# Row-wise largest absolute value of an 8192 x 8192 matrix: GpSimd's shares in two parts, the last row in six pieces, and a store moved to another queue

## Chip, cores, metric

One core of one Trainium2 chip. The metric is the device time of one execution in microseconds (us). Kernels are compared only within the same rounds. A ratio is the mean time of one kernel's fast runs over that of the other's of the same rounds, so it is not quite the ratio of the medians that are quoted.

## The reference

```
x: 8192 x 8192 float32, normally distributed
return np.linalg.norm(x, ord=np.inf, axis=1)      # as used here: the largest |x| of each row
```

The kernel reads 268 MB once and writes 32 KB.

## The kernel before

"Row" below means 128 rows of the matrix, one to each SBUF partition: 8192 columns of float32 on 128 partitions, 4 MB. There are 64 of them: two single ones, 30 pairs, and two single ones at the end. Loads go through a ring of three pairs' size. VectorE reduces each load by itself, except in the last pair and the last two rows: there a share goes to ScalarE (absolute value, in place) and then GpSimd (a maximum over the bits as integers). Each entry of the list is (columns of the piece, columns of them for ScalarE and GpSimd).

```
TILES = (
    [[(8192, 0)]] * HEAD
    + [[(16384, 0)]] * (PAIRS - 1)
    + [[(16384, 7328)], [(8192, 3488)]]
    + [[(4128, 1824), (2048, 864), (1024, 416), (512, 0), (480, 0)]]
)
...
    def absmax_pool(dst, src):
        keep(nc.scalar.activation(src, src, mybir.ActivationFunctionType.Abs))
        max_pool(dst, src)
...
            load = nc.sync.dma_start(out=buf, in_=src[:, off : off + w]).ins
...
            if final:
                pairs_out()                      # two copies on ScalarE, then the store from ScalarE's queue
                absmax(res[:, R - 1 :], last)    # last piece and all partial results of the row
            elif u == len(TILES) - 1:
                for eng, a, e in ((absmax, 0, w - g), (absmax_pool, w - g, w)):
                    ...
                        warm(red, WARM.get(h, ()))   # products that nothing reads
...
    nc.tensor.transpose(ps_ones, res[:, X_ONE:], ident)
    keep(nc.scalar.copy(sb_ones, ps_ones))
    keep(nc.scalar.dma_start(
        out=out[X_ONE * P :].rearrange("(r p) -> r p", p=P), in_=sb_ones
    ))
```

The results of the 60 paired rows are transposed and stored while the last row comes in; those of the four single rows follow at the end: one transpose on TensorE (PE), one copy, one store.

Of the kernel before, what the change touches and what calls it, by code (L numbers as in the profile page):

```python
# [8 lines left out]
P = 128  # L9
FP32 = mybir.dt.float32  # L10
INT32 = mybir.dt.int32
MAX = mybir.AluOpType.max
X = mybir.AxisListType.X



# [2 lines left out]
HEAD = 2  # L19
PAIRS = 30  # L20
TILES = (
    [[(8192, 0)]] * HEAD
    + [[(16384, 0)]] * (PAIRS - 1)
    + [[(16384, 7328)], [(8192, 3488)]]
    + [[(4128, 1824), (2048, 864), (1024, 416), (512, 0), (480, 0)]]
)
RING = 3 * 16384

# [1 line left out]
WARM = {-2: (4, 4, 4), -1: (4,), 0: (4,), 1: (2,)}  # L30


@with_exitstack
def kernel(
    ctx: ExitStack,
    tc: tile.TileContext,
    x: bass.AP,
    out: bass.AP,
):
    nc = tc.nc  # L40
    n_rows, n_cols = x.shape
    R = n_rows // P
    assert R == 64 and n_cols == 8192

    X_ONE = 2 * PAIRS
    n_ones = R - X_ONE
    keep = tc.keep_in_program_order

    single = ctx.enter_context(tc.tile_pool(name="single", bufs=1))
    psum_pool = ctx.enter_context(tc.tile_pool(name="psum", bufs=1, space=bass.MemoryType.PSUM))  # L50

    ring = single.tile([P, RING], FP32)
    res = single.tile([P, R], FP32)
    ident = single.tile([P, P], FP32)


    n_part_last = sum((w > g) + (g > 0) for w, g in TILES[-1][:-1])
    w_last = TILES[-1][-1][0]
    last = single.tile([P, w_last + n_part_last], FP32)

    ps_warm = psum_pool.tile([P, 4 * P], FP32)

    def absmax(dst, src):
        return keep(nc.vector.tensor_reduce(  # L64
            out=dst, in_=src, axis=X, op=MAX, apply_absolute_value=True,
        )).ins

    def max_pool(dst, src):

        pool = nc.gpsimd  # L70
        keep(pool.add_instruction(  # L71
            mybir.InstTensorReduce(
                name=nc.get_next_instruction_name(),
                ins=[pool.lower_ap(src.bitcast(INT32))],
                outs=[pool.lower_ap(dst.bitcast(INT32))],
                op=MAX,
                axis=X,
            )
        ))

    def absmax_pool(dst, src):
        keep(nc.scalar.activation(src, src, mybir.ActivationFunctionType.Abs))  # L82
        max_pool(dst, src)

    def setup(after):

        tc.add_manual_dep(
            nc.gpsimd.memset(ident, 0.0).ins, after.name,  # L88
            mybir.DependencyInfo(mybir.DependencyClass.Sync, mybir.DependencyReason.DATA),
            reason="not before the first row is in",  # L90
        )
        make_identity(nc, ident, nomemset=True)

    def load_table(after):

        abs_ident = nc.scalar.activation(  # L96
            ident[:, :1], ident[:, :1], mybir.ActivationFunctionType.Abs
        )
        tc.add_manual_dep(
            keep(abs_ident).ins, after.name,  # L100
            mybir.DependencyInfo(mybir.DependencyClass.Sync, mybir.DependencyReason.DATA),
            reason="not before the second row is in",
        )

    def warm(after, widths):

        for w in widths:
            product = keep(nc.tensor.matmul(  # L108
                ps_warm[:, : w * P], lhsT=ident,
                rhs=ident.unsqueeze(1).to_broadcast([P, w, P]), start=True, stop=True,  # L110
            )).ins
            tc.add_manual_dep(
                product, after.name,
                mybir.DependencyInfo(mybir.DependencyClass.Sync, mybir.DependencyReason.DATA),
                reason="not before this piece",
            )

    ps_pairs = [psum_pool.tile([PAIRS, P], FP32, name=f"ps_pairs{r}") for r in range(2)]

    def transpose_pairs():  # L120
        both = res[:, :X_ONE].rearrange("p (g r) -> p g r", r=2)
        for r in range(2):
            keep(nc.tensor.transpose(ps_pairs[r], both[:, :, r], ident))  # L123

    def pairs_out():
        sb = single.tile([PAIRS, P, 2], FP32, name="sb_pairs")
        for r in range(2):
            keep(nc.scalar.copy(sb[:, :, r], ps_pairs[r]))  # L128
        keep(nc.scalar.dma_start(
            out=out[: X_ONE * P].rearrange("(g p r) -> g p r", p=P, r=2), in_=sb  # L130
        ))


    loads = []
    at = 0
    next_pair, next_one = 0, X_ONE
    for u, pieces in enumerate(TILES):
        k = sum(w for w, _ in pieces) // n_cols
        if k == 2:
            row, next_pair = next_pair, next_pair + 2  # L140
        else:
            row, next_one = next_one, next_one + 1
        src = x[row * P : (row + k) * P].rearrange("(p r) m -> p (r m)", r=k)
        off = 0
        n_part = 0
        for h, (w, g) in enumerate(pieces):
            final = u == len(TILES) - 1 and h == len(pieces) - 1
            if final:
                buf = last[:, :w]
            else:  # L150
                if at + w > RING:
                    at = 0
                buf = ring[:, at : at + w]
                at += w
            load = nc.sync.dma_start(out=buf, in_=src[:, off : off + w]).ins  # L155
            if not final:
                if (len(loads) + 4) % 10 < 5:


                    for a, v, earlier in loads:  # L160
                        if a < at and at - w < a + v:
                            tc.declare_no_dep(
                                load, earlier, reason="ordered by the reduces in between",
                            )
                loads.append((at - w, w, load))
            off += w
            if u == len(TILES) - 1 and h == 0:
                transpose_pairs()
            if final:
                pairs_out()  # L170
                absmax(res[:, R - 1 :], last)
            elif u == len(TILES) - 1:
                for eng, a, e in ((absmax, 0, w - g), (absmax_pool, w - g, w)):
                    if a < e:
                        i = w_last + n_part
                        red = eng(last[:, i : i + 1], buf[:, a:e])
                        n_part += 1
                        if eng is absmax:
                            warm(red, WARM.get(h, ()))
            elif g == 0:  # L180
                red = absmax(
                    res[:, row : row + k], buf.rearrange("p (c m) -> p c m", m=n_cols)
                )
                if u == 0:
                    setup(red)
                elif u == 1:
                    load_table(red)
            else:

                part = single.tile([P, 2], FP32, name=f"part{u}")  # L190
                c = w // n_cols - 1
                if c:
                    absmax(res[:, row : row + c], buf[:, : c * n_cols])
                red = absmax(part[:, 0:1], buf[:, c * n_cols : w - g])
                absmax_pool(part[:, 1:2], buf[:, w - g :])
                max_pool(res[:, row + c : row + c + 1], part)
                warm(red, WARM[u - len(TILES) + 1])

    ps_ones = psum_pool.tile([n_ones, P], FP32)
    sb_ones = single.tile([n_ones, P], FP32)  # L200
    nc.tensor.transpose(ps_ones, res[:, X_ONE:], ident)  # L201
    keep(nc.scalar.copy(sb_ones, ps_ones))  # L202
    keep(nc.scalar.dma_start(
        out=out[X_ONE * P :].rearrange("(r p) -> r p", p=P), in_=sb_ones
    ))


# [28 lines left out]
```

## Time and profile before

| | before |
|---|---|
| time, median of the first runs | 628.18 us (628.06 to 628.35) |
| execution that the profile shows | 628.7 us, span 626.92 us |
| load rate over the span | 428 GB/s |
| last pair usable for ScalarE / last reduce starts / ends / span ends | 603.80 / 623.62 / 624.28 / 626.92 us |

The span is what the profile shows of the execution; the time was 1.77 to 1.81 us longer in each execution for which both are known. The profile's page and the chain of waits are read in the prediction below.

### The profile page before, as it was taken

What the parts mean: (1) busy time and instruction counts of PE and PEld (TensorE: products, weight loads), DVE (VectorE), ACT (ScalarE), POOL (GpSimd) and SP (SyncE); (2) the same over time, 40 slices, a digit from 0 to 9 for tenths busy, and PEclk for the clock granted to TensorE, in tenths of its full rate; (3) what the DMA queues carried; (4) which work ended last, traced back from release to release, by engine and by line L of the source; (5) the groups of instructions that cost most, each with busy time, mean ns of one, the idle gap of its engine ahead of it and who ended that gap; (6) DMA issues with size and microseconds to landing.
All of it is one profiled execution on the core that took longest, in us unless ns stands there. A gap on an engine that the chain in (4) does not pass through costs nothing.

```text
span 626.9 us, 203 instructions
## 1 busy us (share of the span) xinstructions
PE 8.8 (1%) x15; PEld 3.3 (1%) x15; DVE 537.1 (86%) x39; ACT 14.7 (2%) x10; POOL 13.5 (2%) x13
## 2 busy tenths in 40 slices
PE   0000000000000000000000000000000000000005
PEld 0000000000000000000000000000000000000002
DVE  1938988889888899888898888988889888899888
ACT  0000000000000000000000000000000000000044
POOL 0000000000000000000000000000000000000007
PEclk9999999999999999999999999999999999999999
DMA  9999999999999999999999999999999999999997
GB/s 370 433 468 401 468 401 443 427 414 456 406 464 401 468 401 468 401 468 401 468 401 468 401 468 401 468 401 468 401 468 401 447 422 439 431 414 456 401 435 303
DMA packets 5525, 268.47 MB, mean 428 GB/s; under 512 B 627, under 2 KB 789, under 8 KB 1045
## 3 DMA queue, kind: packets, MB, share of 16 engines
q1 hardware_dynamic: 5472, 268.44, 99.2%
q10 hardware_dynamic: 53, 0.03, 0.0%
HBM read 268.44 MB, written 0.03 MB: 428 GB/s over the span
## 4 chain that ended last, share of the span: by engine, by line
DMA 70%; DVE 29%; SPq 0%; issue 0%; PE 0%; ACT 0%; DVEq 0%
DMA ring<-in_x_dram 70%; DVE res L64 28%; DVE part L64 1%; DVE last L64 1%; SPq L155 0%; PE ps_ones L201 0%; ACT sb_ones L202 0%; DVEq L64 0%
## 5 line engine op out<-in xcount | busy, mean ns | idle before, releaser
L64 DVE TENSOR_REDUCE res<-ring 128x2 f32<-128x16384 f32 (+1 forms) x32 | 525.4, 16419 | 87.0 <-DMA ring<-in_x_dram 87.0
L82 ACT ACTIVATE ring<-ring 128x7328 f32<-128x7328 f32 (+4 forms) x5 | 12.6, 2523 | 577.0 <-DMA ring<-in_x_dram 577.0
L71 POOL TENSOR_REDUCE part<-ring 128x1 int32<-128x7328 int32 (+1 forms) x2 | 9.4, 4697 | 587.9 <-ACT ring L82 587.9
L108 PE MATMUL ps_warm<-ident 128*128 128x512 f32 (+1 forms) x12 | 8.3, 836 | 614.5 <-DVE part L64 613.5
L108 PEld LDWEIGHTS ps_warm<-ident 128*128 128x128 f32 x12 | 3.0, 279 | 618.8 <-issue 615.5
L64 DVE TENSOR_REDUCE part<-ring 128x1 f32<-128x864 f32 (+1 forms) x2 | 6.1, 3048 | 0.1
L64 DVE TENSOR_REDUCE last<-ring 128x1 f32<-128x2304 f32 (+3 forms) x4 | 5.1, 1342 | 0.0
L71 POOL TENSOR_REDUCE last<-ring 128x1 int32<-128x1824 int32 (+2 forms) x3 | 3.0, 1050 | 0.1
L96 ACT ACT_TABLE_LOAD x1 | 1.3, 1283 | 31.4 <-DVE res L64 31.4
L64 DVE TENSOR_REDUCE res<-last 128x1 f32<-128x487 f32 x1 | 0.7, 660 | 0.1
L88 POOL MEMSET ident<- 128x128 f32 x1 | 0.2, 204 | 21.3 <-DVE res L64 21.3
L128 ACT COPY sb_pairs<-ps_pairs 30x128 f32<-30x128 f32 x2 | 0.4, 251 | 0.0
L71 POOL TENSOR_REDUCE res<-part 128x1 int32<-128x2 int32 x2 | 0.4, 195 | 0.1
L123 PE MATMUL ps_pairs<-ident,res 128*30 128x128 f32 x2 | 0.4, 272 | 0.0
L202 ACT COPY sb_ones<-ps_ones 4x128 f32<-4x128 f32 x1 | 0.3, 254 | 1.8 <-PE ps_ones L201 1.8
masks.py:199 POOL TENSOR_SCALAR_AFFINE_SELECT ident<-ident 128x128 f32<-128x128 f32 x1 | 0.3, 292 | 0.1
L201 PE MATMUL ps_ones<-ident,res 128*4 128x128 f32 x1 | 0.3, 271 | 1.3 <-DVE res L64 1.3
L123 PEld LDWEIGHTS ps_pairs<-ident,res 128*30 128x30 f32 x2 | 0.2, 106 | 0.6 <-POOL part L71 0.3
L96 ACT ACTIVATE ident<-ident 128x1 f32<-128x1 f32 x1 | 0.2, 203 | 0.0
L220 POOL MEMSET const-float32-0.0<- 128x1 f32 x1 | 0.1, 98 | 0.2 <-issue 0.2
L220 POOL MEMSET const-bfloat16-1.0<- 128x1 bf16 x1 | 0.1, 101 | 0.0
L220 POOL MEMSET const-uint8-127<- 128x1 uint8 x1 | 0.1, 101 | 0.0
(2 smaller groups left out, 0.2 us busy)
## 6 DMA issues: line engine op xcount, KB each, us to landing
ring<-in_x_dram SPq DMA_DIRECT2D x3, 4096.0 KB, 21.5
ring<-in_x_dram SPq DMA_DIRECT2D x1, 2064.0 KB, 35.7
ring<-in_x_dram SPq DMA_DIRECT2D x1, 1024.0 KB, 37.6
ring<-in_x_dram SPq DMA_DIRECT2D x1, 512.0 KB, 38.4
ring<-in_x_dram SPq DMA_DIRECT2D x30, 40.8
ring<-in_x_dram SPq DMA_DIRECT2D x1, 256.0 KB, 38.5
last<-in_x_dram SPq DMA_DIRECT2D x1, 240.0 KB, 38.6
out_dram<-sb_pairs ACTq DMA_DIRECT2D x1, 30.0 KB, 1.5
```

What stands on the lines that cost most here:

```text
L64: return keep(nc.vector.tensor_reduce(out=dst, in_=src, axis=X, op=MAX, apply_absolute_value=True,)).ins
L71: keep(pool.add_instruction(mybir.InstTensorReduce(name=nc.get_next_instruction_name(), ins=[pool.lower_ap(src.bitcast(INT32))], outs=[poo ...
L82: keep(nc.scalar.activation(src, src, mybir.ActivationFunctionType.Abs))
L88: nc.gpsimd.memset(ident, 0.0).ins, after.name,
L96: abs_ident = nc.scalar.activation(ident[:, :1], ident[:, :1], mybir.ActivationFunctionType.Abs)
L108: product = keep(nc.tensor.matmul(ps_warm[:, : w * P], lhsT=ident, rhs=ident.unsqueeze(1).to_broadcast([P, w, P]), start=True, stop=True,) ...
L123: keep(nc.tensor.transpose(ps_pairs[r], both[:, :, r], ident))
L128: keep(nc.scalar.copy(sb[:, :, r], ps_pairs[r]))
L201: nc.tensor.transpose(ps_ones, res[:, X_ONE:], ident)
L202: keep(nc.scalar.copy(sb_ones, ps_ones))
L220: nc = _bacc.Bacc("TRN2", target_bir_lowering=False, num_devices=1)
```

## The change

Its intent: shorten the stretch after the last load by giving VectorE less to do on the last rows. GpSimd can take more because its share passes ScalarE in two parts, so that the two engines overlap: on the last pair GpSimd started 6.39 us after ScalarE before (603.80 and 610.19 us). The last row comes in six pieces, the last of them smaller. The pairs' store leaves ScalarE's queue for SP's and becomes the last instruction of the program. The diff, cut to its core (the rest moves definitions and renames):

```
-    + [[(16384, 7328)], [(8192, 3488)]]
-    + [[(4128, 1824), (2048, 864), (1024, 416), (512, 0), (480, 0)]]
+    + [[(16384, (3712, 3680))], [(8192, (2016, 1984))]]
+    + [[(3872, (1696,)), (1952, (832,)), (1024, (416,)), (544, (192,)), (384, ()), (416, ())]]
...
-    def absmax_pool(dst, src):
-        keep(nc.scalar.activation(src, src, mybir.ActivationFunctionType.Abs))
-        max_pool(dst, src)
+    def shared(part, n_part, buf, w, g):
+        a = w - sum(g)
+        red = absmax(part[:, n_part : n_part + 1], buf[:, :a])
+        for i, c in enumerate(g):
+            keep(nc.scalar.activation(buf[:, a : a + c], buf[:, a : a + c], ABS))
+            max_pool(part[:, n_part + 1 + i : n_part + 2 + i], buf[:, a : a + c])
+            a += c
+        return red
...
-        keep(nc.scalar.dma_start(
-            out=out[: X_ONE * P].rearrange("(g p r) -> g p r", p=P, r=2), in_=sb
-        ))
...
+    nc.sync.dma_start(
+        out=out[: X_ONE * P].rearrange("(g p r) -> g p r", p=P, r=2), in_=sb_pairs
+    )
```

More of the change, by code (lines that the diff above doesn't have):

```diff
@@ L13 @@
 X = mybir.AxisListType.X
+ABS = mybir.ActivationFunctionType.Abs
 HEAD = 2
@@ L21 @@
 TILES = (
-    [[(8192, 0)]] * HEAD
-    + [[(16384, 0)]] * (PAIRS - 1)
-    + [[(16384, 7328)], [(8192, 3488)]]
-    + [[(4128, 1824), (2048, 864), (1024, 416), (512, 0), (480, 0)]]
+    [[(8192, ())]] * HEAD
+    + [[(16384, ())]] * (PAIRS - 1)
+    + [[(16384, (3712, 3680))], [(8192, (2016, 1984))]]
+    + [[(3872, (1696,)), (1952, (832,)), (1024, (416,)), (544, (192,)), (384, ()), (416, ())]]
 )
@@ L54, with not_before @@
     ident = single.tile([P, P], FP32)
-    n_part_last = sum((w > g) + (g > 0) for w, g in TILES[-1][:-1])
+    ps_warm = psum_pool.tile([P, 4 * P], FP32)
+    ps_pairs = [psum_pool.tile([PAIRS, P], FP32, name=f"ps_pairs{r}") for r in range(2)]
+    sb_pairs = single.tile([PAIRS, P, 2], FP32)
+    ps_ones = psum_pool.tile([n_ones, P], FP32)
+    sb_ones = single.tile([n_ones, P], FP32)
+    n_part_last = sum((w > sum(g)) + len(g) for w, g in TILES[-1][:-1])
     w_last = TILES[-1][-1][0]
     last = single.tile([P, w_last + n_part_last], FP32)
-    ps_warm = psum_pool.tile([P, 4 * P], FP32)
+    def not_before(inst, other, why):
+        tc.add_manual_dep(
+            inst.ins, other.ins.name,
+            mybir.DependencyInfo(mybir.DependencyClass.Sync, mybir.DependencyReason.DATA),
+            reason=why,
+        )
     def absmax(dst, src):
@@ L65, in absmax @@
             out=dst, in_=src, axis=X, op=MAX, apply_absolute_value=True,
-        )).ins
+        ))
     def max_pool(dst, src):
@@ L79, in max_pool @@
         ))
-    def absmax_pool(dst, src):
-        keep(nc.scalar.activation(src, src, mybir.ActivationFunctionType.Abs))
-        max_pool(dst, src)
-    def setup(after):
-        tc.add_manual_dep(
-            nc.gpsimd.memset(ident, 0.0).ins, after.name,
-            mybir.DependencyInfo(mybir.DependencyClass.Sync, mybir.DependencyReason.DATA),
-            reason="not before the first row is in",
-        )
+    def shared(part, n_part, buf, w, g):
[6 more added lines that the diff above has]
+        return red
+    def setup(after):
+        not_before(nc.gpsimd.memset(ident, 0.0), after, "not before the first row is in")
         make_identity(nc, ident, nomemset=True)
     def load_table(after):
-        abs_ident = nc.scalar.activation(
-            ident[:, :1], ident[:, :1], mybir.ActivationFunctionType.Abs
-        )
-        tc.add_manual_dep(
-            keep(abs_ident).ins, after.name,
-            mybir.DependencyInfo(mybir.DependencyClass.Sync, mybir.DependencyReason.DATA),
-            reason="not before the second row is in",
+        not_before(
+            keep(nc.scalar.activation(ident[:, :1], ident[:, :1], ABS)),
+            after, "not before the second row is in",
         )
@@ L107, in warm @@
         for w in widths:
-            product = keep(nc.tensor.matmul(
-                ps_warm[:, : w * P], lhsT=ident,
-                rhs=ident.unsqueeze(1).to_broadcast([P, w, P]), start=True, stop=True,
-            )).ins
-            tc.add_manual_dep(
-                product, after.name,
-                mybir.DependencyInfo(mybir.DependencyClass.Sync, mybir.DependencyReason.DATA),
-                reason="not before this piece",
-            )
-    ps_pairs = [psum_pool.tile([PAIRS, P], FP32, name=f"ps_pairs{r}") for r in range(2)]
-    def transpose_pairs():
-        both = res[:, :X_ONE].rearrange("p (g r) -> p g r", r=2)
-        for r in range(2):
-            keep(nc.tensor.transpose(ps_pairs[r], both[:, :, r], ident))
-    def pairs_out():
-        sb = single.tile([PAIRS, P, 2], FP32, name="sb_pairs")
-        for r in range(2):
-            keep(nc.scalar.copy(sb[:, :, r], ps_pairs[r]))
-        keep(nc.scalar.dma_start(
-            out=out[: X_ONE * P].rearrange("(g p r) -> g p r", p=P, r=2), in_=sb
-        ))
+            not_before(
+                keep(nc.tensor.matmul(
+                    ps_warm[:, : w * P], lhsT=ident,
+                    rhs=ident.unsqueeze(1).to_broadcast([P, w, P]), start=True, stop=True,
+                )),
+                after, "not before this piece",
+            )
     loads = []
@@ L166 @@
             off += w
-            if u == len(TILES) - 1 and h == 0:
-                transpose_pairs()
             if final:
-                pairs_out()
+                for r in range(2):
+                    keep(nc.scalar.copy(sb_pairs[:, :, r], ps_pairs[r]))
                 absmax(res[:, R - 1 :], last)
             elif u == len(TILES) - 1:
-                for eng, a, e in ((absmax, 0, w - g), (absmax_pool, w - g, w)):
-                    if a < e:
-                        i = w_last + n_part
-                        red = eng(last[:, i : i + 1], buf[:, a:e])
-                        n_part += 1
-                        if eng is absmax:
-                            warm(red, WARM.get(h, ()))
-            elif g == 0:
+                if h == 0:
+                    both = res[:, :X_ONE].rearrange("p (g r) -> p g r", r=2)
+                    for r in range(2):
+                        keep(nc.tensor.transpose(ps_pairs[r], both[:, :, r], ident))
+                red = shared(last, w_last + n_part, buf, w, g)
+                n_part += 1 + len(g)
+                warm(red, WARM.get(h, ()))
+            elif not g:
                 red = absmax(
@@ L188 @@
             else:
-                part = single.tile([P, 2], FP32, name=f"part{u}")
+                part = single.tile([P, 1 + len(g)], FP32, name=f"part{u}")
                 c = w // n_cols - 1
@@ L193 @@
                     absmax(res[:, row : row + c], buf[:, : c * n_cols])
-                red = absmax(part[:, 0:1], buf[:, c * n_cols : w - g])
-                absmax_pool(part[:, 1:2], buf[:, w - g :])
+                red = shared(part, 0, buf[:, c * n_cols :], n_cols, g)
                 max_pool(res[:, row + c : row + c + 1], part)
-                warm(red, WARM[u - len(TILES) + 1])
-    ps_ones = psum_pool.tile([n_ones, P], FP32)
-    sb_ones = single.tile([n_ones, P], FP32)
+                warm(red, WARM.get(u - len(TILES) + 1, ()))
     nc.tensor.transpose(ps_ones, res[:, X_ONE:], ident)
@@ L205 @@
     ))
+    nc.sync.dma_start(
+        out=out[: X_ONE * P].rearrange("(g p r) -> g p r", p=P, r=2), in_=sb_pairs
+    )
 _INS = ['x']
```

## The prediction

> **What bounds the kernel now.** I read the page first, then the chain of work that ended last in order of time, then the timeline of the last 25 us, then the busy time by stage. The page says that the kernel is a stream of loads: the transfer engines are busy in nearly every slice and everything else but VectorE is idle.
>
> ```profile
> PE 8.8 (1%) x15; PEld 3.3 (1%) x15; DVE 537.1 (86%) x39; ACT 14.7 (2%) x10; POOL 13.5 (2%) x13
> ...
> DMA  9999999999999999999999999999999999999997
> ...
> HBM read 268.44 MB, written 0.03 MB: 428 GB/s over the span
> ...
> L64 DVE TENSOR_REDUCE res<-ring 128x2 f32<-128x16384 f32 (+1 forms) x32 | 525.4, 16419 | 87.0 <-DMA ring<-in_x_dram 87.0
> ```
>
> VectorE waits 87 us for loads and a 17.22 us reduce of a pair is shorter than the 19.35 us between pairs (565.02 to 584.37 in the timeline). So until the last pieces arrive, nothing that an engine does matters, and the change leaves those loads alone. What it can move is the tail: from the landing of the single row near 613.4 us to the end at 626.9 us. The chain's end shows what is in it:
>
> ```profile
> 582.27 31.14 DMA ring<-in_x_dram
> 613.41 0.03 issue
> 613.43 5.05 DVE part L64
> 618.49 5.05 DVE last L64 x4
> 623.54 0.04 DVEq L64
> 623.57 0.05 issue
> 623.62 0.67 DVE res L64
> 624.29 0.04 issue
> 624.34 0.28 PE ps_ones L201
> 624.62 0.02 issue
> 624.65 0.25 ACT sb_ones L202
> ```
>
> The reader is to see that from 613.43 us on VectorE never waits for a load: it runs six reduces end to end, then PE, ScalarE and the small store follow. VectorE is therefore what bounds the tail, although loads bound the rest. The next view, the timeline, shows how far the loads are ahead: ScalarE is idle between pieces, so its start is the moment a piece is usable.
>
> ```profile
> 613.43 5.05 DVE L64 TENSOR_REDUCE part<-ring 128x1 f32<-128x4704 f32 x1
> 613.48 3.11 ACT L82 ACTIVATE ring<-ring 128x3488 f32<-128x3488 f32 x1 [3.37 <-DMA ring<-in_x_dram]
> 618.33 1.73 ACT L82 ACTIVATE ring<-ring 128x1824 f32<-128x1824 f32 x1 [1.74 <-DMA ring<-in_x_dram]
> 620.74 0.92 ACT L82 ACTIVATE ring<-ring 128x864 f32<-128x864 f32 x1 [0.68 <-DMA ring<-in_x_dram]
> 621.97 0.55 ACT L82 ACTIVATE ring<-ring 128x416 f32<-128x416 f32 x1 [0.30 <-DMA ring<-in_x_dram]
> ```
>
> The last piece was issued at 584.53 us and took 38.6 us to land (the page's DMA issues), so at 623.13 us. VectorE begins the last reduce at 623.62 us, half a microsecond later. **That 0.49 us is all that rebalancing can win**; the load stream and the 3.3 us after the last reduce's start stay.
>
> [...] 8192 columns in 8686 ns and 864 in 1043 ns give 7643/7328 = 1.043 ns. [...] Here the fixed part is 8686 - 8533 = 153 ns for a reduce alone, but from start to start in a row it is only about 0.06 us: 2304 columns start at 618.40 us and 1184 columns at 620.86 us, 2.46 us for 2.40 us of columns.
>
> [...] 7328 columns in 6295 ns, 3488 in 3099 ns, so 0.832 ns a column plus some 0.19 us. ScalarE's pass before it is the same, 6310 and 3109 ns.
>
> [...] The trace of before has no such store to compare; it shows ScalarE's issue at 0.64 us.
>
> **The change part by part.**
>
> *Last row in six pieces, shares re-cut.* First the loads. ScalarE's starts give 618.33 - 613.48 = 4.85 us for 4128 columns, 2.41 for 2048, 1.23 for 1024; landings of the last two, 512 and 480, follow to 623.13. That fits about 1.175 ns a column plus 0.025 us a piece (estimated from these). With the new sizes, added to 613.48: usable at 618.05 (3872), 620.37 (1952), 621.60 (1024), 622.26 (544), 622.74 (384), and the final 416 near 623.25. One more piece costs 0.025 us of landing.
>
> Now VectorE, with 1.0417 ns a column plus 0.06 us, starting each reduce when both the engine and the piece are ready. VectorE starts some 0.05 us before ScalarE on a landed piece, which I use for the loads' times.
> Single row, 8192 - 4000 = 4192 columns: 613.43 + 4.37 + 0.07 = 617.87; the first piece is there at 618.00, so VectorE waits 0.13.
> 2176 columns: 618.00 + 2.27 + 0.06 = 620.33, piece there at 620.32.
> 1120: +1.23 = 621.56, piece at 621.55.
> 608: +0.69 = 622.25, piece at 622.21.
> 352: +0.43 = 622.68, piece at 622.69.
> 384, with its whole end: 622.69 + 0.40 + 0.145 = 623.24; then 0.09 us of waiting for its own results as before (623.53 to 623.62): final start 623.33, last piece there at 623.21.
> Final reduce of 416 + 9 partial results = 425 columns: 0.443 + 0.153 = 0.60 us, end at 623.92 against 624.28 before. **Gain 0.36 us.** Of it 0.06 comes from the shorter final reduce (425 for 487 columns), the rest from 0.53 us less VectorE work on the single row, of which the wait of 0.13 and the added instruction take part back.
>
> *Shares pass ScalarE in two parts.* ScalarE and GpSimd work one after the other on a share; halving lets them overlap. Pair: ScalarE 3.30 us from 603.80, GpSimd starts near 607.2 instead of 610.19 and does 3.28 + 3.25, so it ends near 613.7 instead of 616.48, with 64 more columns. Single: ScalarE's first part ends at 615.36, GpSimd ends its second near 619.1, combine 619.4, against 620.06 before. In the last row GpSimd follows at ScalarE's heels: 1696 from 619.7, 832 to about 622.1, 416 to about 622.6, 192 to about 623.0. The final reduce starts at 623.33, so GpSimd has about 0.3 us to spare and this part wins nothing directly: it pays for the larger share taken off VectorE. Three added ScalarE passes and three added GpSimd passes of about 0.2 us fixed cost each lie beside VectorE's work.
>
> *Pairs' store on SP's queue.* Takes 0.64 us of issue (622.86 to 623.50) off ScalarE, whose next work waits for PE until 624.65; so it wins nothing. On SP it can start when the two copies end, near 622.95; with 1.5 us from issue to landing as before it is in at about 624.5, before the last store, which lands near 625.7. So it lies hidden.
>
> Sum: -0.36 us on the chain; span 626.9 - 0.36, near 626.5; time 628.19 - 0.34, so 627.85 us.
>
> **The rivals.**
> (1) *Landings bind and the lockstep slips.* VectorE is within 0.01 to 0.04 us of each piece's landing; a little slower delivery of small pieces would make it wait five times. The floor is the last landing plus the final reduce, 623.21 + 0.60 + what slips. Landings later by 0.2 us would leave a gain of about 0.2: 628.0. For it: the small pieces deliver a little slower per column (the last 992 in about 1.21 us, 1.22 ns each, where 4128 took 1.175). Against: VectorE has 0.12 us in hand at the last.
> (2) *GpSimd becomes the last wait.* Its chain has four dependent hand-overs from ScalarE in 5 us; if each takes 0.1 us more than I have, its last part ends near 623.4 and the gain falls to about 0.2 us. For it: a slack of only 0.3 us. Against: before, with the longer serial chain, GpSimd still ended at 623.17, 0.4 us before it was needed.
> (3) *The store now ends the program.* If SP's queue handles the store late, behind its loads, or the program's end waits in another order for the queues, the span would be longer: 628.3 to 628.7. For it: SP's last wait is the end of the program and one wait has changed place. Against: SP issues its last load before 586 us and is free for 37 us, and the store has over 1 us to spare.
> [...]
>
> **Range and chances.** No rival reaches even 0.2% of the time, and the runs of before spread over 0.3 us (628.06 to 628.35), with the profiled run at 628.7. The gain is certain to be lost in a 2% verdict. I take 627.85, with a range from 627.3 (runs that came out fast) to 628.4 (rival 3, or slow runs). Faster by over 2% would need 12.6 us, almost the whole tail: 0.5%. Slower by over 2%: 0.5%. Within: 99%.
>
> **What would show it right or wrong.** In the chain of the changed kernel, the last single-row reduce should take about 4.5 us and be followed by a short wait for a load; the final reduce should start at 623.3 us and be 425 columns at about 0.60 us; the last GpSimd part should end by 623.0; the store of the pairs should be issued by SP near 623.0 and not be in the chain. Wrong: a final reduce that starts after 623.5, with GpSimd or a load as its releaser (rivals 2, 1); a later end although VectorE ended at 623.9 (rival 3); or a first landing of the single row away from 613.4 us, which would mean that the loads' rate changed, which I take as fixed.

1.0417 ns a column is what the trace of before gives: 17219 ns for VectorE's reduce of 16384 columns and 8686 ns for one of 8192, so 8533 ns for 8192 columns, and 153 ns more for the reduce. Where the cuts leave a paragraph short: the columns that open the first are VectorE's, those of 7328 and 3488 columns GpSimd's, and "such store" is one on SP's queue.

## The result, and the profile after

628.26 us (628.08 to 628.42, six runs) against 628.18 us before: ratio 1.0001, 95% interval 0.9988 to 1.0014. The time lies inside the stated range, but that range (627.3 to 628.4 us) holds the time of before as well, so it says nothing about the gain. The 0.34 us that I had expected does not show, and a part of this study is about where it went.

The chain of waits of the changed kernel, its end (columns: start, length in us, what):

```profile
582.41 35.40 DMA ring<-in_x_dram
617.82 0.02 issue
617.84 5.35 DVE last L75 x5
623.19 0.03 DVEq L75
623.22 0.05 issue
623.27 0.61 DVE res L75
623.88 0.04 issue
623.92 0.36 PE ps_ones L189
...
624.31 0.26 ACT sb_ones L190
```

Before, the last wait for a load in the chain ended at 613.41 us, with the single row. Now it ends at 617.82 us, with the last row's first piece: VectorE finished the single row early and waits for a load, as predicted. The timeline of the same kernel:

```profile
617.84 1.62 ACT L97 ACTIVATE ring<-ring 128x1696 f32<-128x1696 f32 x1 [0.94 <-DMA ring<-in_x_dram]
...
619.52 3.43 POOL L82 TENSOR_REDUCE last<-ring 128x1 int32<-128x1696 int32 x4 [0.38 <-ACT ring L97]
620.20 0.90 ACT L97 ACTIVATE ring<-ring 128x832 f32<-128x832 f32 x1 [0.74 <-DMA ring<-in_x_dram]
...
621.51 1.01 ACT L97 ACTIVATE ring<-ring 128x416 f32<-128x416 f32 x2 [0.41 <-DMA ring<-in_x_dram]
...
622.85 0.42 SPq L194 DMA_DIRECT2D out_dram<-sb_pairs  x1
```

GpSimd ends at 619.52 + 3.43 = 622.95 us, 0.32 us before the last reduce, and the pairs' store is issued at 622.85 us, long before the last one: no rival there.

Absolute times of two executions mislead here, because the load stream itself ends a little earlier or later in each. So I measure the tail from ScalarE's first start on the last pair, here before and then after:

```profile
603.80 6.31 ACT L82 ACTIVATE ring<-ring 128x7328 f32<-128x7328 f32 x1 [570.88 <-DMA ring<-in_x_dram]
```

```profile
603.58 6.46 ACT L97 ACTIVATE ring<-ring 128x3712 f32<-128x3712 f32 x2 [570.46 <-DMA ring<-in_x_dram]
```

From there to the end of the last reduce: 624.28 - 603.80 = 20.48 us before, 623.87 - 603.58 = 20.29 us after. **The gain in the chain is 0.19 us, where I had predicted 0.36.** From there to the span's end it is 23.12 and 23.03 us, a gain of only 0.09. The difference is in PE and the store. The busy time by stage around the last transpose, before and then after (columns: stretch and its length, busy us of PE, PEld, DVE, ACT and POOL with counts, granted clock, transfer share, GB/s):

```profile
624.30:624.70 0.40, 0.27 (x1) 0.08 (x1) 0.00 (x0) 0.05 (x1) 0.00 (x0) 1.00 0.00 0
```

```profile
623.90:624.30 0.40, 0.35 (x1) 0.08 (x1) 0.00 (x0) 0.00 (x0) 0.00 (x0) 0.61 0.02 5
```

In this one execution the granted clock fell during the transpose, to a mean of 0.61 over that stretch where it was 1.00 before, and the transpose took 0.35 us instead of 0.27. That did not recur: it took 0.27 or 0.28 us in all twelve later looks, two of them at this same kernel (e2, e9). So 0.08 us of the loss belongs to that execution, not to the change.

### The profile page after: what moved, and what is told of

It is laid out like the page before. It is cut to its first block, busy times and chain, and to the rows that moved or that the text cites. A ratio compares the mean times of both kernels' runs of the same rounds, so it can differ in the third digit from the quotient of the medians.

```text
span 626.6 us, 212 instructions
## 1 busy us (share of the span) xinstructions
PE 8.1 (1%) x15; PEld 3.0 (0%) x15; DVE 536.8 (86%) x40; ACT 15.6 (2%) x13; POOL 14.6 (2%) x16
## 4 chain that ended last, share of the span: by engine, by line
DMA 71%; DVE 28%; SPq 0%; issue 0%; PE 0%; ACT 0%; DVEq 0%
DMA ring<-in_x_dram 71%; DVE res L75 28%; DVE last L75 1%; SPq L147 0%; PE ps_ones L189 0%; ACT sb_ones L190 0%; DVEq L75 0%
## 5 line engine op out<-in xcount | busy, mean ns | idle before, releaser
L97 ACT ACTIVATE ring<-ring 128x3712 f32<-128x3712 f32 (+7 forms) x8 | 13.5, 1712 | 575.9 <-DMA ring<-in_x_dram 572.6
L82 POOL TENSOR_REDUCE part<-ring 128x1 int32<-128x3712 int32 (+3 forms) x4 | 10.1, 2563 | 586.0 <-ACT ring L97 586.0
L75 DVE TENSOR_REDUCE part<-ring 128x1 f32<-128x800 f32 (+1 forms) x2 | 5.5, 2748 | 0.1
L75 DVE TENSOR_REDUCE last<-ring 128x1 f32<-128x2176 f32 (+4 forms) x5 | 5.3, 1115 | 0.1
L82 POOL TENSOR_REDUCE last<-ring 128x1 int32<-128x1696 int32 (+3 forms) x4 | 3.3, 842 | 0.5 <-ACT ring L97 0.4
## 6 DMA issues: line engine op xcount, KB each, us to landing
ring<-in_x_dram SPq DMA_DIRECT2D x30, 40.8
```

The costliest lines, as they stand in the source:

```text
L75: return keep(nc.vector.tensor_reduce(out=dst, in_=src, axis=X, op=MAX, apply_absolute_value=True,))
L82: keep(pool.add_instruction(mybir.InstTensorReduce(name=nc.get_next_instruction_name(), ins=[pool.lower_ap(src.bitcast(INT32))], outs=[poo ...
L97: keep(nc.scalar.activation(buf[:, a : a + c], buf[:, a : a + c], ABS))
```

## The experiments

Twelve runs on three chips: e1 to e4 on one, e5 to e8 on the second, e9 to e12 on the third. First the readings from their profiles, since the timed differences are close to the scatter. A "look" is one profiled execution. "Start" is ScalarE's first start on the last pair; the next two columns count from it. "Landing" is from the single row's completion to the last piece's, read from the trace's records of when a load's sixteenth and last part has reported.

| run | start | last reduce starts | ends | from there to span end | landing |
|---|---|---|---|---|---|
| before, first look | 603.80 | 19.82 | 20.48 | 2.64 | 9.75 |
| e1 before again | 603.28 | 19.82 | 20.48 | 2.63 | 9.77 |
| e3 before, store on SP | 603.23 | 19.82 | 20.48 | 2.70 | 9.77 |
| after, first look | 603.58 | 19.69 | 20.29 | 2.75 | 9.92 |
| e2 after again | 603.30 | 19.67 | 20.27 | 2.67 | 9.91 |
| e9 after again | 603.30 | 19.65 | 20.25 | 2.66 | 9.88 |
| e4 after, store on ScalarE | 603.37 | 19.66 | 20.26 | 2.61 | 9.89 |
| e5 before, half | 603.25 | 19.51 | 20.17 | 2.65 | 9.79 |
| e6 after, half | 603.38 | 19.63 | 20.22 | 2.67 | 9.89 |
| e7 before, first piece as four loads | 603.47 | 19.92 | 20.58 | 2.76 | 9.96 |
| e8 after, even cuts | 603.24 | 19.80 | 20.43 | 2.67 | 10.04 |
| e10 after, odd cuts | 603.24 | 19.56 | 20.16 | 2.67 | 9.78 |
| e11 even cuts, SBUF place shifted | 603.33 | 19.53 | 20.16 | 2.65 | 9.79 |
| e12 re-cut | 603.33 | 19.53 | 20.13 | 2.67 | 9.80 |

The two middle columns repeat to 0.04 us for one kernel, while the start scatters by over 0.5 us although every program's loads are the same up to there. A tail change of 0.2 us is therefore plain in these columns and blurred in a time.

### Both kernels again (e1, e2)

No edit in either.

> The unchanged kernel of before against itself, to see what its usual execution looks like. Theory A (the profiled execution of before, 628.7 us, was an unusually late one, since the six timed ones ran from 628.06 to 628.35): ratio 1.0000, median 628.2, the profiled span 626.2 to 626.5 instead of 626.9, no pair interval longer than 19.40 us in the load stream. Theory B (626.9 us was the usual span, and the change shortens the span but something outside it gives the time back): span again near 626.9 with a time near 628.2.

Measured: 628.26 us, before in the same rounds 628.37, ratio 0.9999 (0.9986 to 1.0011); span 626.39 us; no interval between pairs over 19.40 us. Theory A holds for the look at before: the first one was unusual. The chain of waits shows where, in its early part. First look at before:

```profile
59.25 41.08 DMA ring<-in_x_dram
...
117.60 41.03 DMA ring<-in_x_dram
```

The changed kernel's first look at the same places:

```profile
59.46 40.80 DMA ring<-in_x_dram
...
117.53 40.80 DMA ring<-in_x_dram
```

Later links of both chains are 40.8 us. So the load stream of that execution lost 0.28 and 0.23 us at two places, far from anything the change touches. Comparing the two first spans (626.92 and 626.62) would have shown the predicted gain for the wrong reason.

> The changed kernel once more, on the same chip. Theory A: ratio to before 0.9999 to 1.0003 as in the first result, span 626.3 to 626.6, and the stretch from the single row's first reduce to the end as long as in the new look at before, within 0.15 us. Theory B: span 0.3 us or more below that of e1. The transpose of the last rows takes either 0.27 or 0.35 us.

Measured: 628.05 us (627.96 to 628.15) against 628.37 us (628.17 to 628.66), ratio 0.9995 (0.9983 to 1.0008). All five runs lie below all nine of before. The span is 0.15 us below e1's. Neither theory as I had put them: the change does gain, about 0.2 us, which the first result did not show. The tail (20.27 + 2.67) is 0.16 us shorter than e1's.

### The store by itself (e3, e4)

e3 puts the store of the pairs last on SP's queue in the kernel before:

```
-        keep(nc.scalar.dma_start(out=out[: X_ONE * P]..., in_=sb))
...
+    nc.sync.dma_start(out=out[: X_ONE * P]..., in_=sb_pairs)     # after the last store
```

> The kernel before with one part of the change alone: the pairs' store is issued by SP as the last instruction of the program. If the store is hidden, as predicted: ratio 1.0000 within 0.0002. Theory C (the store on SP's queue costs at the end of the program what the re-cut wins): +0.3 us, ratio 1.0005, with a longer stretch from the last store's issue to the span's end than 2.0 us.

Measured: 628.36 us, ratio 1.0000 (0.9987 to 1.0012). e4 puts it back on ScalarE's queue in the changed kernel, the same edit reversed.

> The changed kernel with the pairs' store back on ScalarE's queue, so the re-cut alone. Theory C: -0.3 us against the kernel before, 627.85. Theory A (re-cut wins less than 0.15 us, because from the single row on the loads and not VectorE set the pace): 628.1 to 628.3, the same as the changed kernel within 0.1 us.

Measured: 628.05 us, the same as the changed kernel's 628.05 of the same rounds; ratio 0.9995 (0.9981 to 1.0008). Theory C, that the store costs what the re-cut wins, falls. A small cost is there. The last store's issue in e3 and in e4, from their timelines:

```profile
624.36 0.55 ACTq L201 DMA_DIRECT2D out_dram<-sb_ones  x1
```

```profile
624.27 0.26 ACTq L194 DMA_DIRECT2D out_dram<-sb_ones  x1
```

With the pairs' store on SP, the last store is the first that ScalarE's queue issues, and its issue takes 0.55 us; as the second it takes 0.26. In all fourteen looks the first store on that queue took 0.54 to 0.64 us to issue and the second 0.26 to 0.27 us. Most of this is hidden; the stretch from the last reduce to the span's end grows from 2.63 to 2.70 us (e1, e3) and falls from 2.67 to 2.61 us (e2, e4). Single looks stray in this stretch (e7, with the store on ScalarE, has 2.76), and over all fourteen looks the medians are 2.64 us with the pairs' store on ScalarE and 2.67 us with it on SP. So the move loses some 0.03 to 0.06 us instead of nothing. That the dearer issue is the reason, and not the changed order of the last instructions, is likely but was not tested apart.

### What sets the pace of the tail (e5, e6)

VectorE reduces only half of its share in the pieces of the last row but the last one. A maximum that lies in the other half is missed; the comparison with the reference passed all the same, so it is no proof for such a run.

```
-                        red = eng(last[:, i : i + 1], buf[:, a:e])
+                        half = e // 2 if eng is absmax else e
+                        red = eng(last[:, i : i + 1], buf[:, a:half])
```

> The kernel before, with VectorE reducing only the first half of its share in the first four pieces of the last row (2304 columns less, 2.4 us of VectorE work; the result is wrong on purpose where a row's largest value lies in what is left out). If VectorE bounds the tail of before by 0.4 us over the landings, as predicted: 0.25 to 0.45 us less than before, because the last reduce then starts at the last landing or at GpSimd's last part. If the loads bound it already: no change.

Measured: 627.90 us against 628.28, ratio 0.9997 (0.9983 to 1.0011, with one late run of 628.75 among the five). In the profile the last reduce ends 0.31 us earlier. The end of its chain now begins with the load of the last piece (landed at 622.63 us), and the timeline names that load as what the reduce waited for:

```profile
622.63 0.03 issue
622.66 0.05 DVEq L64
622.71 0.05 issue
622.76 0.67 DVE res L64
```

```profile
622.76 0.66 DVE L64 TENSOR_REDUCE res<-last 128x1 f32<-128x487 f32 x1 [0.28 <-DMA last<-in_x_dram]
```

VectorE bounded the tail of before, with 0.31 us over the loads; the prediction had put that at 0.49. In the changed kernel the same edit is made in `shared`.

> The same in the changed kernel (2320 columns less for VectorE in the first five pieces). Theory A (the loads' landings now set the pace of the tail): at most 0.15 us less than the changed kernel, so 627.9 to 628.05 where that has 628.05. Rival (VectorE still bounds the tail as before): another 0.3 to 0.4 us less, about 627.7.

Measured: 628.22 us against 628.28 on this chip, where the changed kernel itself was not timed; as a time it misses both expectations. The profile decides: with 2.4 us of VectorE work gone, the last reduce starts 19.63 us after the start, against 19.65 to 19.69 in the changed kernel. Its last reduces now wait for loads:

```profile
621.92 0.83 DVE L75 TENSOR_REDUCE last<-ring 128x1 f32<-128x176 f32 x2 [0.19 <-DMA ring<-in_x_dram]
...
623.01 0.60 DVE L75 TENSOR_REDUCE res<-last 128x1 f32<-128x425 f32 x1 [0.26 <-DMA last<-in_x_dram]
```

So in the changed kernel the loads set the pace, with only some 0.04 us of VectorE on top. And they come later than before: 9.88 to 9.92 us after the single row instead of 9.75 to 9.77, for the same 4 MB.

### What one more piece costs (e7)

```
+            if w == 4128:      # four loads of 1032 columns in place of one
+                for i in range(3):
+                    nc.sync.dma_start(out=buf[:, i * 1032 : (i + 1) * 1032], in_=src[...])
+                load = nc.sync.dma_start(out=buf[:, 3096:], in_=src[...]).ins
```

> The kernel before with the load of the last row's first piece cut into four loads of 1032 columns; the reduces stay as they are. It prices one more piece in the load stream. As I had it in the prediction, 0.025 us a piece: the last landing comes 0.08 us later after that of the single row (9.75 us before). Rival, from the looks at the changed kernel, where six pieces landed 0.15 us later than five: 0.08 to 0.15 us a piece, so 0.25 to 0.45 us later in all, and the time rises by most of what exceeds 0.45 us of slack, or not at all.

Measured: landing 9.96 us, 0.19 later than e1 for three more loads, 0.06 us each; the last reduce starts 0.10 us later; 628.53 us against 628.28, ratio 1.0004 (0.9992 to 1.0017). Between my two figures, and it decides nothing, because these pieces also begin at new places, which turned out to matter (9.79 us against 10.04 in e11 and e8).

### Where the cuts lie (e8, e10, e11)

e8 keeps six pieces but moves all cuts to multiples of 64 columns (256 bytes):

```
-    + [[(3872, (1696,)), (1952, (832,)), (1024, (416,)), (544, (192,)), (384, ()), (416, ())]]
+    + [[(3840, (1664,)), (1984, (864,)), (1024, (416,)), (512, (160,)), (384, ()), (448, ())]]
```

> The changed kernel with the cuts of its last row moved to multiples of 64 columns (3840, 1984, 1024, 512, 384, 448), still six pieces. If where a piece begins in its row accounts for the later landing: single row to last landing back at 9.80 us or less, and 0.1 us faster than the changed kernel. If the number of pieces accounts for it: 9.87 to 9.92 us as in the changed kernel, and the same time within 0.1 us.

Measured: landing 10.04 us, later than either expectation; the last reduce ends 0.14 to 0.18 us later than in the changed kernel, of which 0.03 us is that it is longer (457 columns for 425); 628.22 us, ratio 1.0002 (0.9989 to 1.0014). So the place matters here, and the "round" places are the slow ones of these runs. Counted in units of 32 columns (128 bytes), the cuts of before are 129, 193, 225 and 241, all odd; those of the changed kernel 121, **182**, **214**, 231 and 243, two of them even; those of e8 all even. (The last row begins at column 24576 of the ring, an even place, so cuts that are odd in the row are odd in SBUF too; the last piece has a tile of its own.) The single loads agree: 1024 columns took 1.23 us from landing to landing in before, where they begin at 193, but 1.28 to 1.31 us in the changed kernel, where they begin at 182. The trace's packets do too, as far as they go: all 128 packets of 4096 bytes took 159 ns in before, and from 159 to 172 ns in e8 and in the changed kernel. Their mean rose only by 1 to 2% (160.7 ns in the changed kernel, 161.8 ns in e8), the time of the load by about 5%, so longer packets are not shown to be the whole of it.

e10 moves only the two even cuts of the changed kernel by 32 columns. VectorE's part of every piece stays as it is (1120 of the second, 352 of the fourth).

```
-    + [[(3872, (1696,)), (1952, (832,)), (1024, (416,)), (544, (192,)), (384, ()), (416, ())]]
+    + [[(3872, (1696,)), (1984, (864,)), (1024, (416,)), (512, (160,)), (384, ()), (416, ())]]
```

> The changed kernel a third time, as the base for the other three on this chip. From the landing of the last pair to the end of VectorE's last reduce 20.42 us, single row to last landing 9.90 us, as in the other looks at it; 0.05 to 0.3 us below before in the timed runs.

> The changed kernel with two of its five cuts moved, so that every cut lies at an odd multiple of 32 columns (3872, 5856, 6880, 7392, 7776), as in the kernel before; in the changed kernel two lay at even ones (5824, 6848), in the aligned one all. If the place of the cuts accounts for part of the late landing: single row to last landing 9.80 to 9.85 us against 9.90, loads of 1024 columns 1.23 us against 1.29, and the chain 0.05 to 0.1 us shorter. If the count of six pieces alone accounts for it: 9.90 us again.

Measured: e9, the changed kernel: 628.04 us (628.00 to 628.24) against 628.24 (628.12 to 628.39), ratio 0.9998 (0.9986 to 1.0011); landing 9.88 us, as in the other looks at it. Its expected 20.42 us counts from the last pair's landing: the records of the sixteenth part give 20.35. e10: landing 9.78 us, the load of 1024 columns 1.22 us, the last reduce ends 0.09 us earlier than in e9. The timed median, 628.09 us (627.87 to 628.45; ratio 0.9999, 0.9985 to 1.0013), does not show it; this run is carried by its profile alone. ScalarE's starts on the second and third piece, in e8 and then in e10:

```profile
619.89 0.92 ACT L97 ACTIVATE ring<-ring 128x864 f32<-128x864 f32 x1 [0.84 <-DMA ring<-in_x_dram]
...
621.17 1.01 ACT L97 ACTIVATE ring<-ring 128x416 f32<-128x416 f32 x2 [0.36 <-DMA ring<-in_x_dram]
```

```profile
619.80 0.93 ACT L97 ACTIVATE ring<-ring 128x864 f32<-128x864 f32 x1 [0.72 <-DMA ring<-in_x_dram]
...
621.03 0.96 ACT L97 ACTIVATE ring<-ring 128x416 f32<-128x416 f32 x2 [0.30 <-DMA ring<-in_x_dram]
```

Both executions have their start at 603.24 us and both loads bring 1024 columns; 1.28 us lie between the two starts in e8 and 1.23 in e10.

Up to here a piece moves in its row in HBM and in SBUF together. e11 takes e8's even cuts and shifts only the SBUF side:

```
+        if u == len(TILES) - 1:
+            at += 32          # the last row begins 32 columns further on in the ring
```

> The aligned version (10.04 us from single row to last landing), with the place of the last row in SBUF moved by 32 columns, so that source cuts stay at even multiples of 32 columns and SBUF places become odd ones. If the SBUF side matters: back to 9.85 us or less, up to the last piece, which has its own tile. If the place in the row in HBM matters: 10.0 us again.

Measured: landing 9.79 us against e8's 10.04, with the same cuts in HBM; 627.95 us (627.90 to 628.05) against 628.24, ratio 0.9996 (0.9983 to 1.0008). Here the SBUF side decides. The runs do not show why, nor any cost of the cuts' places in HBM: six pieces landed after 9.78 us with cuts at odd multiples of 128 bytes there (e10) and after 9.79 us with even ones (e11). Places are counted from the start of the row and of the ring, whose own addresses are not in the trace. The two looks are on different chips, but the changed kernel's cuts landed after 9.89 us on the one (e6) and 9.88 us on the other (e9). The first piece of e11, which begins at an odd place too for once, landed after 4.54 us against 4.59 in e8.

### A version from this (e12)

Cuts all odd (119, 183, 215, 233, 243), and sizes and shares worked out anew with the measured durations, so that VectorE, GpSimd and the last landing meet.

```
-    + [[(16384, (3712, 3680))], [(8192, (2016, 1984))]]
-    + [[(3872, (1696,)), (1952, (832,)), (1024, (416,)), (544, (192,)), (384, ()), (416, ())]]
+    + [[(16384, (3712, 3680))], [(8192, (2240, 1856))]]
+    + [[(3808, (1536,)), (2048, (880,)), (1024, (448,)), (576, (240,)), (320, ()), (416, ())]]
```

> A re-cut from what the runs showed: six pieces of 3808, 2048, 1024, 576, 320 and 416 columns with all cuts at odd multiples of 32, GpSimd's shares 1536, 880, 448, 240, and 4096 of the single row in two parts. Worked out with the measured landings and durations: last pair's landing to the end of the last reduce 20.26 us, against 20.42 in the changed kernel and 20.62 in before; so 0.16 us below the changed kernel and 0.36 below before in the timed runs, as far as the load stream's own scatter of 0.15 us lets it be seen.

Measured: 627.86 us (627.79 to 627.98) against 628.24 (628.12 to 628.39) before and 628.04 for the changed kernel; ratio 0.9994 (0.9982 to 1.0007). All five runs lie below all nine of before and all five of the changed kernel. The expected 20.26 us counts from the last pair's landing, not from the table's start, so its differences are what can be compared: 0.16 us below the changed kernel and 0.36 below before were expected, 0.12 (e9) and 0.35 (e1) are in the table. The end of its chain:

```profile
617.49 5.27 DVE last L75 x5
...
622.86 0.61 DVE res L75
```

Within 2% it is the "same" as both; the interval of the ratio, which is wider than the differences here, includes 1. The pairs' store on ScalarE's queue (e4) was not combined with it; by the looks at the store above that may give another 0.03 to 0.06 us (an estimate).

## Why the prediction was right, and where it was not

**What bounds the tail: right, with too much room.** VectorE bounded the tail of before; e5 shows it, with 0.31 us to win, not the 0.49 that I called all that rebalancing can win. The step that was off is the hand-over from the last landing to the last reduce: 0.03 + 0.05 + 0.05 = 0.13 us in e5's chain, where I had taken 0.05 us at most. That leaves 0.36 us. Of the rest, 0.03 us is my reading of the last landing: 623.13 us from the page's rounded time to landing, 623.16 us by its sixteenth part. And in e5 the last piece landed 0.03 us later, counted from the start (19.39 us for 19.36).

**Single row and shares: right.** VectorE waits for the first piece of the last row, GpSimd ends 0.32 us before it is needed (I had 0.3), and each new instruction has the duration that I worked out (VectorE 4192 columns 4520 ns, the last reduce 595 ns for my 0.60 us).

**The landings: the term that was mis-sized.** I let the sixth piece add 0.025 us and put the last landing 9.77 us after the single row. It came after 9.88 to 9.92 us. VectorE, which I had in lockstep within 0.01 to 0.04 us of the landings, was held back with them: the last reduce started 19.65 to 19.69 us after the start instead of 19.53. That is rival 1 of the prediction, with another cause than the one I gave it. The count of pieces costs what I had assumed: six pieces with odd cuts land after 9.78 us, five after 9.75 to 9.77. The rest, 0.1 us and more, is the place of two cuts (e10), and by e11 their place in SBUF. (I had read the first piece's 4.85 us from ScalarE's starts; between landings it is 4.90, since ScalarE started 0.07 us after the single row's landing and 0.02 us after the next. My fit had the sum right nevertheless: 9.77 us for the 9.78 that e10 shows.) With these mended and VectorE's work left as it was, the last reduce starts at 19.56 and ends at 20.16 us, where I had 19.53 and 20.12.

**The store: nearly right.** Hidden as predicted, but 0.03 to 0.06 us dearer, probably because the last store is now the first on its queue (e3, e4). Rival 3 had 0.1 to 0.5 us for it, and a late end of SP's queue as the cause; neither was seen.

**The last transpose.** It was slower in the first look, 0.35 us at a granted clock of 0.61, and took 0.27 or 0.28 us in the twelve later looks.

**Two signs in absolute times.** The last reduce started at 623.27 us, and I had said 623.3. That was luck: the stream of this look was 0.22 us ahead, and counted from the start the reduce came 0.16 us late. And the single row landed at 613.19 us, not at 613.4, which my sign would have called a changed rate of the loads; the interval from the last pair's landing to it was 9.72 us, against 9.71 before.

**The sum.** Chain -0.19 to -0.23 us, store +0.03 to +0.06, so -0.13 to -0.20 us instead of -0.36; the whole tail was 0.16 us (e2) and 0.20 us (e9) shorter than e1's. In two sets of rounds the timed medians agree in sign: -0.32 us (e2) and -0.20 us (e9), though the intervals of both ratios include 1. In the first result they do not: +0.08 us. The start of the tail in fourteen looks spread from 603.23 to 603.80 us with the same loads before it, and one transpose ran at the lower clock (0.61, 0.08 us longer); that could cover it, but why the first six runs of the changed kernel were later than the ten of e2 and e9, I cannot show.

## What to carry to other kernels

Where loads set the pace, as here, the end could be shortened only down to the last landing (with 2.4 us less VectorE work the last reduce came 0.31 us earlier in e5, and at most 0.06 us in e6), and a balance worked out to hundredths of a microsecond is worth what the landing times in it are worth: measure them with the new sizes, not with the old. When a load is cut, the cuts' places are a parameter of their own (in these runs six pieces of one row landed after 9.78 to 10.04 us); the kernel before had good ones without saying so, and the change lost them. For differences smaller than the scatter of the stream, compare a stretch of the profile that begins after the stream, in several looks, and not two spans.
